# The last stage of a retrieval block: splits made in four column quarters, and another order of the sorted blocks

## The chip, the cores and the metric

The kernel runs on one core of one Trainium2 chip. Its time is the device time of one execution in microseconds (us), and the number that counts is the median over executions. The core has a matrix engine (PE, with PEld for the loads of its stationary operand), a vector engine (DVE), a scalar engine (ACT), GpSimd (POOL) and a queue engine (SP). SP and ACT start plain transfers between main memory and the on-chip memory SBUF; POOL starts the gathers whose row numbers are read from an on-chip table. Sixteen DMA engines move the bytes. Matrix products are summed in PSUM, in eight banks of 128 partitions by 512 fp32 numbers.

## The reference

The reference is one layer of an encoder on 256 tokens of width 2048: a mixer (short convolutions and latent attention) and then a retrieval FFN with 16384 single-neuron experts. Only the last part bears on this change. For each token eight heads choose 16 experts each, and

```python
u = u_tab[ids]
a = jnp.einsum('td,tnd->tn', hx, u)
act = jax.nn.gelu(a, approximate=False) * g
return jnp.einsum('tn,tnd->td', act, v_tab[ids])
```

The result is scaled by a gate, added to the residual `x`, and normalised: `y = RMSNorm(x + gate2 * PEER(h2))`.

## The kernel before

The table `u` is not gathered. All 128 blocks of 128 experts are multiplied with all tokens (main loop, `i1` from 0 to 127), the activations are weighed with the gates, and they are stored as rows of a table `actd`, one row of 256 tokens for each expert. Then comes the last stage, which this change touches.

For the product with `v` the kernel sorts the experts by which of eight groups of 32 tokens use them. The sorted list is cut into 109 blocks of 128 experts. For each block POOL issues one gather of 128 rows of `peer_v` (1 MB; tiles `rv`, `rvd`, `rvg`, `early`, `A`; line 1355) and one of the rows of `actd` that belong to them (128 KB, or 64 KB when only one half of the tokens needs the block; tiles `mc`, `mcs`; line 1366). These two alternate in POOL's queue, in the order of the table `ORDER`. Each gather waits for the eighth gather before it to have landed, and a gather into a reused tile waits for the last reader of that tile: a matrix product, or a split on DVE.

`plan()` turns `ORDER` into 89 turns of the matrix engine, numbered 0 to 88. A block is needed by groups of tokens; the tokens are in two halves (0 and 1). A turn is one of three kinds. A full turn multiplies all 128 tokens of one half with one block; it runs on reduced-precision operands, so the block and its activations are first split into a high and a low part, and the turn is three passes (high times high, low times high, high times low) of four products, one for each column quarter of 512. A pair turn takes two pieces of 64 tokens, a single turn four pieces of 32 tokens, in fp32 without a split. Half 0 is summed in the banks `po0` to `po3`, half 1 in `po4` to `po7`. Four blocks (`DEFER`) need only half 1, fully; they stand at the end of the turns as turns 85 to 88, and 86 to 88 are run column quarter by column quarter (`po4` first, all three turns, then `po5`, and so on).

The split is `split_to` (lines 245 to 247): ACT copies the source into the high part (line 246), then DVE subtracts the high part from the source (line 247). There are three pairs of split buffers (`hwhi0/hwlo0`, `hwhi1/hwlo1`, `hboth`), and two more (`hx`) near the end. `prepare` (line 1467) splits the block and then its activations (`mhl`); a fourth wait comes with that: a split waits until the full turns that used the pair are done.

After the turns, `finish` (line 1565) does for each half: product times gate into a temporary (1569), add to the residual (1570), square with a running sum on ACT (1571), the mean and the reciprocal root on 128 single numbers (1573 to 1579), multiplication with the weight `g_final` (1582), scaling by the root (1586 on ACT, 1588 on DVE), and two stores. The residual rows are loaded by SP (1544) into the tile `early` when its two halves are no longer needed for gathers, and `g_final` (1548) into the tile of an `rv` that was split.

The program's text is not the order on an engine: a scheduler places instructions of DVE and ACT by priority and by its own view of when operands are ready, so instructions of `finish` can stand ahead of a split. The products of the last stage and the gathers are kept in the order of the text. Each engine runs its own queue in order.

Of the kernel before, what the change touches and what calls it, by code (L numbers as in the profile page):

```python
# [44 lines left out]
NSORT = 109  # L45
PLACES = 256
SHIFT = 14
ORDER = (57, 86, 85, 47, 59, 106, 53, 58, 42, 98, 102, 1, 101, 34, 77, 8, 55, 16, 88, 10, 76, 5, 83, 107, 105,
# [4 lines left out]
DEFER = (78, 79, 80, 81)  # L53
SORT_FROM = 51
SORT_SIDE = 3.6
# [36 lines left out]
def plan():  # L92
# [3 lines left out]
    for m, n in rows + [(255, 128 * NSORT - BASE3)]:  # L96
        for b in range(at // 128, (at + n - 1) // 128 + 1):
            need[b] |= m
        at += n
    assert sorted(ORDER) == list(range(NSORT))  # L100
    assert all(need[b] == 240 for b in DEFER)
    turns, pairs, singles = [], [[], []], [[] for _ in range(4)]

    def emit(kind, lanes):
        turns.append([x.pop(0) + (kind,) for x in lanes if x])

    for n, b in enumerate(ORDER):
        for tt in range(2):
# [14 lines left out]
        for kind, lanes in (("pair", pairs), ("single", singles)):  # L123
            while all(lanes) or any(x and (last or x[0][0] <= n - HELD) for x in lanes):
                emit(kind, lanes)
    turns += [[(n, 1, "full")] for n, b in enumerate(ORDER) if b in DEFER]
    return turns, [need[b] for b in ORDER]

# [39 lines left out]
def hybrid_block_kernel(  # L168
# [53 lines left out]
    def keep(x):  # L222
        tc.keep_in_program_order(x)
        return x
# [20 lines left out]
    def split_to(src, hi, lo):  # L245
        S.activation(hi, src, AF.Copy)  # L246
        V.tensor_tensor(lo, src, hi.bitcast(F32), ALU.subtract)
# [1103 lines left out]
    def index(b):  # L1351
        return bass.IndirectOffsetOnAxis(ap=perm[:, b:b + 1], axis=0)

    def fetch_raw(kind, raw):
        keep(nc.gpsimd.indirect_dma_start(raw, None, v_rows, index(ORDER[len(raws)])))  # L1355
        raws.append(raw)
        kinds.append(kind)

    def fetch_m(m):
        n = len(ms)  # L1360
        to, at, rows = m, actd[:, :], index(ORDER[n])
        for h in range(2):
# [101 lines left out]
    def first(slots, ok=lambda x: True):  # L1464
        return slots.pop(min((x[0], k) for k, x in enumerate(slots) if ok(x))[1])

    def prepare(n, raw, m, gs):
        at, (hi, lo) = first(wide)
        also, k = first(narrow)
        mh, ml = mhl[:, 2 * k], mhl[:, 2 * k + 1]  # L1470
        ready[n] = max([at, also, taken.get(n, -1) + LANDS] + list(ready.values())) + 1.5
        split_to(raw, hi, lo)
        ts_ = slice(32 * gs[0], 32 * gs[-1] + 32)
        split_to(m[:, ts_], mh[:, ts_], ml[:, ts_])
        split[n] = (hi, mh), (lo, mh), (hi, ml)
        live.append((turn_of[1][n] if n >= 0 else -1, (hi, lo), k))

    for i in range(TAIL):
        m = ab[-1][:, ABLK - TAIL + i]
        if i:  # L1480
            prepare(-1, tails[i], m, range(8))
        for tt in range(2):
            for r, mm in split[-1] if i else [(tails[i], m)]:
                for d4 in range(4):
                    product(r, mm, tt, 128, d4, start=(i == 0))
# [14 lines left out]
    while i < len(turns):  # L1500
# [13 lines left out]
        while more:  # L1514
            more = False

            def usable(x):
                return not (x[1] == "T2" and len(raws) >= T2_STOP or x[1][0] == "W" and len(raws) >= W_STOP)

            if len(ms) < len(raws) and m_free:  # L1520
                fetch_m(first(m_free)[-1])
                more = True
            elif len(ms) == len(raws) < min(NSORT, now + AHEAD + 1) and any(map(usable, raw_free)):
                place = first(raw_free, usable)
                taken[len(raws)] = place[0]
                fetch_raw(*place[1:])
                more = True
            if seen < min(len(ms), now + SPLIT_AHEAD + 1) and (turn_of[1][seen] < 0 or wide and narrow):
                if turn_of[1][seen] >= 0:
                    prepare(seen, raws[seen], ms[seen], full_halves[seen])  # L1530
                held.append(seen)
                seen += 1
                more = True
            for n in [n for n in held if turn_of[0][n] < i]:
                held.remove(n)
                key = max(turn_of[0][n], ready.get(n, -1))
                raw_free.append((key, kinds[n], raws[n]))
                m_free.append((key, ms[n]))
                more = True
# [159 lines left out]
```

## Time and profile before

| | us |
|---|---|
| median of 3 executions | 1682.59 |
| lowest and highest | 1680.96, 1696.75 |
| the profiled execution | 1661.88 |
| its span | 1660.1 |
| matrix products of the last stage begin | 1314.9 |
| last gather issued by POOL | 1621.7 |
| split of the last gathered block begins on ACT | 1632.8 |
| last matrix product ends | 1646.3 |
| last arithmetic ends, last store is issued | 1654.5 |

The profile is of one execution, about 20 us shorter than the median of the others. In its rows L1444 is the line of all products of the last stage, whatever the kind of the turn, L246 and L247 are the two halves of a split, and a name such as `rv` stands for all tiles of that name. A row of the timeline gives the start, the duration and, in brackets, how long the engine had been idle and what ended that. A row with "x2" is two instructions merged into one row.

### The profile page before, as it was taken

To read this page: it belongs to the slowest core of one execution; us is meant where nothing else is said; L and a number is where in the kernel's file an instruction comes from. 1 tells how busy PE (TensorE), PEld (TensorE's weight loads), DVE (VectorE), ACT (ScalarE), POOL (GpSimd) and SP (SyncE) were. 2 spreads that over 40 slices of the span, in tenths; PEclk is the share of its full clock that TensorE was granted. 3 is DMA by queue.
4 is the path that set the end of the run, shared out by engine and by line. 5 is a ranking of instruction groups with operands and counts; after the bars stand their busy time and mean duration, and the time that the engine had idled before them with its cause. 6 is when DMAs were issued, how large, how long until landed. Compare 5 with 4: busy or idle time off the path is not lost.

```text
span 1660.1 us, 29785 instructions
## 1 busy us (share of the span) xinstructions
PE 1582.7 (95%) x12776; PEld 1384.5 (83%) x12780; DVE 1114.5 (67%) x1496; ACT 696.3 (42%) x787; POOL 471.4 (28%) x356
## 2 busy tenths in 40 slices
PE   3999999999999999999999999999999999898995
PEld 2779899999999999999999999999999866444432
DVE  5778778877777889998997866576675434123215
ACT  3225457534544446654664333434343333122113
POOL 0000000000000000000000006888885378777770
PEclk9999999999999999999999999999999999999997
DMA  9996988889665556655668779999999899999994
GB/s 394 426 418 234 348 330 328 302 307 339 233 244 178 185 203 204 232 201 205 253 225 286 237 270 268 288 358 359 341 354 397 297 344 363 388 400 381 374 417 198
DMA packets 115722, 502.52 MB, mean 303 GB/s; under 512 B 13392, under 2 KB 55888, under 8 KB 60288
## 3 DMA queue, kind: packets, MB, share of 16 engines
q1 hardware_dynamic: 44640, 319.79, 52.0%
q0 software_dynamic: 25184, 129.25, 20.2%
q10 hardware_dynamic: 45760, 51.51, 9.7%
q8 instruction: 102, 1.67, 0.4%
q14 instruction: 36, 0.29, 0.0%
HBM read 462.57 MB, written 37.94 MB: 301 GB/s over the span
## 4 chain that ended last, share of the span: by engine, by line
PE 79%; DVE 7%; DMA 6%; issue 3%; POOL 3%; ACT 2%; SPq 0%; DVEq 0%; ACTq 0%; POOLq 0%
PE pu L257 12%; PE pu L258 12%; PE pu L263 12%; PE po L1444 10%; PE pin L748 4%; PE pwin L257 2%; PE pwin L258 2%; PE pwin L263 2%; PE gps L1043 2%; PE pwout L257 2%; PE pwout L258 2%; PE pwout L263 2%; PE pq L258 2%; PE pq L257 2%; PE pq L263 2%
## 5 line engine op out<-in xcount | busy, mean ns | idle before, releaser
L257 PE MATMUL pu<-h2hi,hu 128*128 128x256 f32 x2048 | 479.7, 279 | 2.8 <-ACT hu L239 2.8
L239 ACT ACTIVATE hu<-ru 128x2048 fp32r<-128x2048 f32 x128 | 245.8, 1921 | 394.3 <-PE pu L258 291.2
L240 DVE TENSOR_TENSOR lu<-ru,hu 128x2048 fp32r<-128x2048 f32 x128 | 292.6, 2287 | 165.9 <-ACT hu L239 159.3
L257 PEld LDWEIGHTS pu<-h2hi,hu 128*128 128x128 f32 x2048 | 384.9, 188 | 3.5 <-ACT hu L239 3.2
L263 PE MATMUL pu<-h2hi,lu 128*128 128x256 f32 x2048 | 254.0, 277 | 0.9 <-DVE lu L240 0.9
L1320 POOL DMA_DIRECT2D gg<-gd x3 | 3.9, 1289 | 882.6 <-DMA permd<-pad 882.6
L1288 POOL DMA_INDIRECT permd<-work x126 | 207.0, 1643 | 148.7 <-DVE work L1284 110.6
L258 PE MATMUL pu<-h2loT3b,hu 128*128 128x256 f32 x1024 | 247.3, 278 | 0.0
L263 PEld LDWEIGHTS pu<-h2hi,lu 128*128 128x128 f32 x2048 | 242.1, 188 | 1.1 <-DVE lu L240 1.1
L258 PE MATMUL pu<-h2loT3a,hu 128*128 128x256 f32 x1024 | 240.4, 277 | 0.0
L258 PEld LDWEIGHTS pu<-h2loT3b,hu 128*128 128x128 f32 x1024 | 192.7, 188 | 0.2 <-issue 0.2
L258 PEld LDWEIGHTS pu<-h2loT3a,hu 128*128 128x128 f32 x1024 | 192.4, 188 | 0.0
L1444 PE MATMUL po<-rv,mc 128*32 128x512 f32 (+1 forms) x336 | 92.5, 604 | 0.0
L240 DVE TENSOR_TENSOR lwin<-rwin,hwin 128x2048 fp32r<-128x2048 f32 x33 | 75.5, 2288 | 22.2 <-ACT hwin L239 21.0
L1444 PE MATMUL po<-rv,mcs 128*32 128x512 f32 (+1 forms) x312 | 85.0, 600 | 5.7 <-DMA mcs<-actd,ident 4.3
L1355 POOL DMA_INDIRECT rv<-in_peer_v_dram,perm_idx x66 | 74.8, 1134 | 52.0 <-ACT hwhi L246 29.7
L239 ACT ACTIVATE hwin<-rwin 128x2048 fp32r<-128x2048 f32 x33 | 63.1, 1913 | 56.8 <-PE pin L748 26.6
L1444 PE MATMUL po<-hwhi,mhl 128*128 128x512 f32 x272 | 76.8, 410 | 6.0 <-ACT mhl L246 6.0
L257 PE MATMUL pwin<-hhi,hwin 128*128 128x256 f32 x336 | 81.0, 286 | 0.0
L258 PE MATMUL pwin<-hlo,hwin 128*128 128x256 f32 x336 | 78.7, 279 | 0.0
L1444 PEld LDWEIGHTS po<-hwhi,mhl 128*128 128x128 f32 x272 | 51.7, 194 | 29.0 <-ACT mhl L246 11.1
L284 DVE SCALAR_TENSOR_TENSOR acc<-ada,cact,acc 128x2048 f32<-128x2048 f32 x30 | 70.3, 2344 | 6.4 <-DMA ada<-in_w_ada_dram 6.4
(594 smaller groups left out, 3170.0 us busy)
## 6 DMA issues: line engine op xcount, KB each, us to landing
ru<-in_peer_u_dram SPq DMA_DIRECT2D x128, 1024.0 KB, 6.0
ada<-in_w_ada_dram SPq DMA_DIRECT2D x96, 1024.0 KB, 7.7
rwin<-in_w_in_dram SPq DMA_DIRECT2D x33, 1024.0 KB, 6.7
rwout<-in_w_out_dram SPq DMA_DIRECT2D x16, 1024.0 KB, 6.7
rwq<-in_w_q_dram SPq DMA_DIRECT2D x16, 1024.0 KB, 4.9
gd<-stage ACTq DMA_DIRECT2D x16, 1024.0 KB, 5.2
actd<-A ACTq DMA_DIRECT2D x14, 1024.0 KB, 8.8
gg<-gd ACTq DMA_DIRECT2D x13, 1024.0 KB, 8.0
```

The lines of the kernel that those rows point to most:

```text
L239: S.activation(hi, raw, AF.Copy)
L240: lo_op = V.tensor_tensor(lo, raw, hi.bitcast(F32), ALU.subtract)
L257: PE.matmul(dst, lhsT=whi[:, sl], rhs=rhi[:, c], start=(c == sets[0][0]), stop=False)
L258: PE.matmul(dst, lhsT=whi[:, sl], rhs=rlo[:, c], start=False, stop=False)
L263: PE.matmul(dst, lhsT=wlo[:, sl], rhs=rhi[:, c], start=False, stop=(c == cs[-1] and cs == last))
L284: op = V.scalar_tensor_tensor(acc, raw, cact[:, k:k + 1], acc, ALU.mult, ALU.add)
L748: PE.matmul(dst, lhsT=wt[:, (4 * n + j) * 128:(4 * n + j + 1) * 128], rhs=ht[:, 4 * q + j], start=start, stop=stop, skip_group_check=True)
L1043: keep(PE.matmul(p[:, j * 128:(j + 1) * 128], lhsT=ohs[0][:, t0 + j], rhs=ohs[1][:, t0 + j, c], start=(c == 0), stop=(c == 2)))
L1288: put_one = nc.gpsimd.indirect_dma_start(permd[:, :], bass.IndirectOffsetOnAxis(ap=place[:, i:i + 1], axis=0), ids[:, i:i + 1], None)
L1320: keep((S if 1 < k < NG - 1 else nc.gpsimd).dma_start(gg, gd[:, :, k * ABLK:(k + 1) * ABLK, :].rearrange("tb p i t -> p tb i t")))
L1355: keep(nc.gpsimd.indirect_dma_start(raw, None, v_rows, index(ORDER[len(raws)])))
L1444: keep(PE.matmul(po[tt * 4 + d4][row:row + size], lhsT=m[:, at * size:(at + 1) * size], rhs=raw[:, d4 * 512:(d4 + 1) * 512], start=start, ...
```

## The change

Two things. The split of a block is made in four pieces of 512 columns, each with its own ACT copy and its own DVE subtraction; the split of the activations stays one piece and still follows. And the table `ORDER` is another permutation of the same 109 blocks (same number of full, pair and single turns: 48, 21 and 20; the same bytes). In the new order the last turn that adds to half 0 is turn 82, before it was turn 84.

```diff
-ORDER = (57, 86, 85, 47, 59, 106, 53, 58, 42, 98, 102, 1, 101, 34, 77, 8, 55, 16, 88, 10, 76, 5, 83, 107, 105,
+ORDER = (82, 52, 45, 70, 84, 73, 85, 59, 86, 96, 2, 75, 6, 15, 50, 98, 38, 21, 61, 103, 19, 53, 5, 40, 34, 0,
 ...
         ready[n] = max([at, also, taken.get(n, -1) + LANDS] + list(ready.values())) + 1.5
-        split_to(raw, hi, lo)
+        for d4 in range(4):
+            ds_ = slice(d4 * 512, (d4 + 1) * 512)
+            split_to(raw[:, ds_], hi[:, ds_], lo[:, ds_])
         ts_ = slice(32 * gs[0], 32 * gs[-1] + 32)
         split_to(m[:, ts_], mh[:, ts_], ml[:, ts_])
```

Lines behind the insertion move down by two (1569 becomes 1571, 1582 becomes 1584). What the new order does on the engines shows at three places.

DVE at the end of the stage, before the change: the last two splits (`hwlo0`, `hx01`, with their `mhl`) and the start of `finish`.

```order
L247 TENSOR_TENSOR hwlo0_14790<-rvg_14832,hwhi0_14789 128x2048
L247 TENSOR_TENSOR mhl_14794<-mcs_14795,mhl_14794 128x128
L1569 TENSOR_TENSOR rvg_14832<-po0_14769,gtf_9852 128x512
L1569 TENSOR_TENSOR rvg_14832<-po1_14770,gtf_9852 128x512
L247 TENSOR_TENSOR hx01_16180<-rv4_14224,hx00_16179 128x2048
L247 TENSOR_TENSOR mhl_14794<-mcs_14795,mhl_14794 128x128
L1570 TENSOR_TENSOR early_13637<-early_13637,rvg_14832 128x512 x2
L1569 TENSOR_TENSOR rvg_14832<-po2_14771,gtf_9852 128x512
L1569 TENSOR_TENSOR rvg_14832<-po3_14772,gtf_9852 128x512
```

And after it, from the split of the block of turn 85 on.

```order
L247 TENSOR_TENSOR hwlo1_14792<-rvd1_14779,hwhi1_14791 128x512 x4
L247 TENSOR_TENSOR mhl_14794<-mcs_14795,mhl_14794 128x128
L1571 TENSOR_TENSOR A120_14294<-po0_14769,gtf_9852 128x512
L1571 TENSOR_TENSOR A120_14294<-po1_14770,gtf_9852 128x512
L1572 TENSOR_TENSOR early_13637<-early_13637,A120_14294 128x512 x2
L1571 TENSOR_TENSOR A120_14294<-po2_14771,gtf_9852 128x512
L1571 TENSOR_TENSOR A120_14294<-po3_14772,gtf_9852 128x512
L1572 TENSOR_TENSOR early_13637<-early_13637,A120_14294 128x512 x2
L1575 TENSOR_REDUCE fsum0_16481<-fs0_16479 128x1
L1576 TENSOR_SCALAR fv0_16483<-fsum0_16481 128x1
L1578 RECIPROCAL fr0_16485<-fr0_16485 128x1
```

Behind these stand three more small instructions of half 0, and only then the splits of the last three blocks (`hboth` from `rv6`, `hx01` from `rv7`, `hwlo0` from `rv5`), the four multiplications with `g_final` of half 0, and `finish` of half 1. So the sums and the root of half 0 moved ahead of three splits on DVE, and their squares and the root's ACT part moved ahead of the same splits on ACT.

PE around the last turns with half 0, after the change: `po0` to `po3` end with the third pass of turn 82 (its first and last products are shown), then the pair turn 83 and the single turn 84 add to half 1 alone.

```order
L1444 MATMUL po0_14769<-hwhi0_14789,mhl_14794 128x512
L1444 MATMUL po1_14770<-hwhi0_14789,mhl_14794 128x512
L1444 MATMUL po2_14771<-hwhi0_14789,mhl_14794 128x512
L1444 MATMUL po3_14772<-hwhi0_14789,mhl_14794 128x512
L1444 MATMUL po4_14773<-rv4_14224,mc0_14647 64x512
L1444 MATMUL po4_14773<-early_13637,mcs_14795 64x512
L1444 MATMUL po5_14774<-rv4_14224,mc0_14647 64x512
L1444 MATMUL po5_14774<-early_13637,mcs_14795 64x512
```

Before, the same kind of place was turn 84, a single turn whose pieces go to both halves.

```order
L1444 MATMUL po4_14773<-A120_14294,mc1_14648 32x512
L1444 MATMUL po0_14769<-rv3_14110,mc1_14648 32x512
L1444 MATMUL po4_14773<-rv3_14110,mc1_14648 32x512
L1444 MATMUL po0_14769<-rv7_14527,mcs_14795 32x512
L1444 MATMUL po5_14774<-A120_14294,mc1_14648 32x512
```

POOL in the middle of the stage, after the change: the gathers of the blocks 75 to 79 and of their activations, with the semaphores each waits for.

```order
L1355 DMA rvd1_14779<-in_peer_v_dram,perm_idx_5645 128x2048 [waits DMASW1_49,PE_49]
L1366 DMA mcs_14795<-actd_68,ident_70 128x128 [waits DMASW2_49,DVE_49]
L1355 DMA A120_14294<-in_peer_v_dram,perm_idx_5645 128x2048 [waits DMASW3_49,DVE_49,PE_49]
L1366 DMA mc3_14650<-actd_68,perm_idx_5645 128x256 [waits DMASW4_49]
L1355 DMA rv9_14781<-in_peer_v_dram,perm_idx_5645 128x2048 [waits DMASW5_49,PE_49]
L1366 DMA mcs_14795<-actd_68,perm_idx_5645 128x256 [waits DMASW6_49,DVE_49]
L1355 DMA early_13637<-in_peer_v_dram,perm_idx_5645 128x2048 [waits DMASW7_49,PE_49]
L1366 DMA mcs_14795<-actd_68,ones_71 128x128 [waits DMASW0_49]
L1355 DMA rvd1_14779<-in_peer_v_dram,perm_idx_5645 128x2048 [waits DMASW1_49,DVE_49]
```

The last row gathers block 79 into the tile `rvd1`, into which block 75 was gathered four blocks earlier; it waits on DVE for that block's split. Block 80 goes into the tile of block 76 in the same way. In the old order the shortest such distance was five blocks (42 into the tile of 37, 69 into that of 64).

8 rows, old and new, of the table ORDER are left out of this document.

## The prediction

> **What bounds the kernel now.** First the page's head and the stretches of the last stage (busy time of each engine with its number of instructions, granted clock, DMA share, GB/s).
>
> ```profile
> span 1660.1 us, 29785 instructions
> core 0: us, PE busy (x) PEld busy (x) DVE busy (x) ACT busy (x) POOL busy (x), PEclk, DMA share, GB/s
> 1310.00:1350.00 40.00, 40.00 (x221) 24.50 (x223) 16.15 (x15) 11.78 (x13) 30.63 (x26) 1.00 0.75 260
> 1350.00:1400.00 50.00, 50.00 (x265) 32.81 (x258) 20.29 (x15) 17.81 (x16) 40.25 (x33) 1.00 0.95 363
> 1400.00:1520.00 120.00, 112.24 (x597) 54.22 (x595) 25.34 (x20) 21.86 (x21) 92.65 (x85) 0.97 1.00 398
> 1520.00:1550.00 30.00, 29.10 (x132) 17.45 (x134) 12.60 (x10) 9.34 (x10) 24.82 (x18) 0.91 0.88 334
> 1550.00:1633.00 83.00, 73.36 (x396) 30.54 (x393) 18.75 (x15) 17.22 (x17) 56.20 (x52) 0.96 0.99 401
> 1633.00:1660.10 27.10, 10.63 (x36) 7.52 (x34) 20.72 (x42) 11.27 (x23) 0.00 (x0) 0.72 0.27 110
> ...
> 1309.60:1622.70 313.10, 297.07 (x1566) 156.11 (x1564) 89.74 (x72) 73.94 (x72) 244.85 (x210) 0.97 0.95 371
> ```
>
> Only the last 345 us change. To 1633 the DMA engines are nearly full, but not everywhere: 260, 363 and 334 GB/s stand beside 398 and 401. After 1633 DVE is the busy engine. What holds the DMA back is in POOL's rows (minimum, median and maximum in ns, then a stretch of its timeline) and DVE's for the same time.
>
> ```profile
> L1366 POOL DMA_INDIRECT mc<-actd,perm_idx x29: 942/946/2973, 1312.7 to 1608.7; - x29
> L1366 POOL DMA_INDIRECT mcs<-actd,perm_idx x24: 942/946/3035, 1327.6 to 1581.7; - x24
> POOL mcs L1366 <- issue: 14.9, 49, 0.3
> 1335.13 3.04 POOL L1366 DMA_INDIRECT mcs<-actd,perm_idx  x1 [0.30 <-issue]
> 1338.47 2.24 POOL L1355 DMA_INDIRECT A<-in_peer_v_dram,perm_idx  x1 [0.30 <-issue]
> 1341.01 1.89 POOL L1366 DMA_INDIRECT mcs<-actd,ones  x1 [0.31 <-issue]
> 1343.20 0.95 POOL L1355 DMA_INDIRECT rvg<-in_peer_v_dram,perm_idx  x1 [0.30 <-issue]
> 1351.97 0.94 POOL L1366 DMA_INDIRECT mc<-actd,ident  x1 [0.30 <-issue]
> 1335.06 2.29 DVE L247 TENSOR_TENSOR hwlo<-rv,hwhi 128x2048 fp32r<-128x2048 f32 x1 [1.37 <-ACT hwhi L246]
> 1337.27 0.42 DVE L247 TENSOR_TENSOR mhl<-mcs,mhl 128x256 fp32r<-128x256 f32 x1
> 1337.60 2.28 DVE L247 TENSOR_TENSOR hwlo<-rv,hwhi 128x2048 fp32r<-128x2048 f32 x1
> 1339.80 2.29 DVE L247 TENSOR_TENSOR hboth<-rv,hboth 128x2048 fp32r<-128x2048 f32 x1
> 1352.36 2.29 DVE L247 TENSOR_TENSOR hwlo<-rvd,hwhi 128x2048 fp32r<-128x2048 f32 x1 [1.51 <-ACT hwhi L246]
> ```
>
> Half of the gathers take 0.946 us, with 0.30 us between two. The long ones end 0.8 to 0.9 us behind the end of a wide subtraction: 1338.17 behind 1337.35, 1340.71 behind 1339.88, 1342.90 behind 1342.09. A gather that begins while a subtraction runs waits for its end, then takes its usual time, even though the next subtraction has begun: it slips in between two. The other way round there is no such wait: the subtraction of 1352.36 began inside the gather of 1351.97 and kept its 2.29 us.
>
> POOL's whole time is accounted for: 210 gathers of 0.946 us are 198.7 us, 209 gaps of 0.30 us are 62.7 us, and the busy time of 244.85 us is 46.2 us more than 198.7; sum 307.6 of 313.1 us. So it waits for tiles or landings for 5 us in all. The stage is paced by POOL's issue, of which 46 us is waiting for wide subtractions, and by the DMA engines where POOL runs ahead. Last, the end, from the last block's split on.
>
> ```profile
> 1632.77 1.92 ACT L246 ACTIVATE hx<-rv 128x2048 fp32r<-128x2048 f32 x1 [0.78 <-DMA rv<-in_peer_v_dram,perm_idx]
> 1635.44 2.28 DVE L247 TENSOR_TENSOR hx<-rv,hx 128x2048 fp32r<-128x2048 f32 x1
> 1637.78 1.02 PE L1444 MATMUL po<-hx,mhl 128*128 128x512 f32 x2 [2.34 <-DVE hx L247]
> 1639.05 1.28 DVE L1569 TENSOR_TENSOR rvg<-po,gtf 128x512 f32<-128x512 f32 x2
> 1642.31 1.28 ACT L1575 ACT_TABLE_LOAD   x1
> 1643.98 1.28 DVE L1569 TENSOR_TENSOR rvg<-po,gtf 128x512 f32<-128x512 f32 x2
> 1645.48 0.85 PE L1444 MATMUL po<-hx,mhl 128*128 128x512 f32 x3
> 1648.51 1.28 DVE L1570 TENSOR_TENSOR early<-early,rvg 128x512 f32<-128x512 f32 x2
> 1653.37 1.15 ACT L1586 ACTIVATE early<-early,fr 128x1024 f32<-128x1024 f32 x1 [0.81 <-DVE fr L1579]
> 1654.55 0.36 ACTq L1589 DMA_DIRECT2D out_dram<-early  x1
> ```
>
> Call L the landing of the last block, 1632.8. PE's last product ends at 1646.3, L+13.6; the last arithmetic at 1654.5, L+21.7; the span at L+27.3. DVE begins half 1 only at 1643.98, because the sums of half 0 and a split stood in its queue before that.
>
> **The change part by part.** The first and the last wide subtraction of POOL's time, and the durations of a split's pieces:
>
> ```profile
> 1309.73 2.29 DVE L247 TENSOR_TENSOR hwlo<-rvd,hwhi 128x2048 fp32r<-128x2048 f32 x1 [1.52 <-ACT hwhi L246]
> ...
> 1615.83 2.29 DVE L247 TENSOR_TENSOR hwlo<-rvd,hwhi 128x2048 fp32r<-128x2048 f32 x1 [5.42 <-ACT hwhi L246]
> ...
> L246 ACT ACTIVATE mhl<-mcs x19: 289/294/420, 1332.8 to 1634.6; 128x128 fp32r<-128x128 f32 x12, 128x256 fp32r<-128x256 f32 x7
> L246 ACT ACTIVATE hwhi<-rv x9: 1894/1911/1915, 1333.1 to 1534.3; 128x2048 fp32r<-128x2048 f32 x9
> L247 DVE TENSOR_TENSOR hwlo<-rvd,hwhi x7: 2291/2291/2294, 1309.7 to 1615.8; 128x2048 fp32r<-128x2048 f32 x7
> ```
>
> *One split.* ACT's copy grows by (1.911-0.294)/1920 us a column, so 512 columns take 0.62 us, and four some 2.3 us instead of 1.9. Two 512-wide DVE operations last 1.28 us and the next row shows the same shape 1.2 us on, so 0.60 us each: four are 2.4 instead of 2.29 us. But a quarter's subtraction follows its own copy: the low part is ready about 3.0 us after the landing instead of 4.3. The high part of the activations, which ACT makes after the copies, comes 0.4 us later. PE meets both; off the end this moves nothing, as POOL's queue sets the pace. [...]
>
> *POOL's waits.* 35 wide subtractions lie between 1309.7 and 1622.7 (the first and the last are quoted above), so each costs POOL 1.3 us. Four quarters keep DVE busy for 2.4 us, in which POOL, at 1.25 us plus a wait, begins about 1.5 gathers; each waits for the rest of one quarter, 0.30 us on average. That is 0.46 us a split, 16 us in all: 30 us saved in POOL's queue. Bounds: 46 us if no gather meets a quarter badly; 4 us if two gathers wait a whole quarter each time (2x0.60x35 = 42).
>
> *What of it reaches the end.* With POOL ahead, the DMA engines are next. From 1350 to 1633 the rows give 363x50+398x120+334x30+401x83 = 109.2 MB; at 400 GB/s (the two full stretches) that takes 273 us instead of 283: 10 us. From 1310 to 1350 small gathers come first and POOL's rate counts; of the three waits shown (2.1, 1.3 and 0.9 us), a third would stay: some 2 us of the 40. So L comes 12 us earlier. Bounds: nothing (400 GB/s is only reached where it was), and 20 us, if the faster POOL fills the DMA as in its best stretches.
>
> *The order.* Same blocks, same bytes, same kinds of turns. It could make PE late or starve it; the trace of before cannot show it, so I bound it by the stage's PE slack: PE was busy 73.36 of the last 83 us and 112.24 of 120, some 17 us idle. I take 0, with 5 us either way. The gather that waits for a split only four blocks back (block 79) has three blocks in flight before it, 1.1 MB each at 400 GB/s, 8 us; its split needs 3. Nothing is lost there.
>
> *The end.* Half 0 is complete at turn 82; eight 512-wide DVE operations (4.8 us), a square on ACT, the 1.28 us table load and a few small ones, 8 us in all, now run before the last three blocks land. Before, blocks came 2.8 us apart at the end (1.1 MB at 400 GB/s), so block 101, which turn 82 needs, lands near L-20 and turn 82 ends near L-15: room for 8 us before the split at L-5.6. In queue behind this on DVE and ACT are the last three splits, and PE behind those; if the cover were gone, each us late costs one at the end. Then: last split ready at L+3.3 (was 1637.7, L+5.0); PE needs the 8.5 us it took from 1637.78 to 1646.3, so L+11.8; meanwhile DVE does `g_final` for half 0 and half 1's first columns. After the last product: product, one `g_final` piece and sum, 1.8 us; from the last sum to the end of arithmetic 4.0 us (4.7 before, from 1649.8 to 1654.5, with more `g_final` pieces in it); the store 5.5 us as before. L+23, not L+27.3: 4.5 us, between 2 and 6.
>
> Sum: 12+4.5 = 16.5 us: 1661.9 becomes 1645.4 for a profiled execution, and carried over as the same number of us, the median 1682.6 becomes 1666. Why the median lies 20 us above the profiled execution the trace doesn't show.
>
> **The rivals.**
>
> 1. *Only the end is gained.* The DMA share of 0.95 from 1309.6 to 1622.7 can be read as full already: POOL then merely waits for landings instead of subtractions. For it: 0.99 to 1.00 at 398 and 401. Against it: 260, 363 and 334 GB/s where the long gathers crowd. L gains 0 to 4, the end 4.5: 1676. [...]
>
> 2. *More is gained.* POOL's 30 us reach L nearly whole, the DMA running above 401 GB/s: L-20, end -6: 1657.
>
> 3. *Slower: gathers and quarters take turns.* If whichever begins first holds off the other, each quarter can wait for a gather, three more waits a split of about half of 0.94 us: 1.4 us a split. POOL gains nothing, since it waits for each quarter. Splits on the path pay: those that PE waited for
>
> ```profile
> PE po L1444 <- ACT mhl L246: 8.1, 3, 4.4
> PE po L1444 <- DVE hwlo L247: 2.9, 4, 0.9
> ```
>
> seven times 1.4, and three at the end, 14 us, less 4.5: 1692. It decides if a quarter's duration grows beyond 0.7 us. Against it stands the subtraction of 1352.36.
>
> **How the numbers follow.** Forecast 0.60, rival 1 0.22, rival 2 0.10, rival 3 0.08. The forecast's own range is 1659 to 1675 (L by 5 to 18, the end by 2 to 6). For 8 in 10 I take 1651 to 1681: it holds the first three, with a few us for the spread of the medians (1680.96 to 1696.75). A measurement tells about 1% from no change, 1665.8 to 1699.4 here; the forecast lies on that line. Over 1% faster: 0.10 from rival 2, half of the forecast, 0.04 from rival 1 by spread: 0.45. Slower by over 1% needs rival 3 and more: 0.06. The rest, 0.49, is within.
>
> **What would show it.** POOL's gathers longer than 1.6 us are gone and its busy time over them falls from 245 to about 215 us; 260, 363 and 334 GB/s rise towards 400; the last gather is issued 12 us sooner. Squares of half 0 stand before the splits of the last three blocks, the table load off the path, the end at L+23. Wrong: POOL's mean gather unchanged; quarters of 0.7 us or more; new POOL waits on PE; the half-0 sums running after L.

## The result, and the profile after

The changed kernel's median is 1686.94 us (1678.27 to 1842.26, 21 executions), that of the kernel before 1680.96 us in the same comparison (1666.70 to 1698.75, 21 executions). The ratio is 1.0063 with a 95% interval of 1.0040 to 1.0086: slower, by about 11 us by the ratio and 6 us by the medians. Slow executions, such as the one of 1842.26 us, are left out of the ratios here and below. The forecast was 1666, with a range of 1651 to 1681. The profiled execution of the changed kernel took 1684.45 us, close to its median.

First the head of its page, and then the stretches, with the columns of the prediction: busy time of PE, PEld, DVE, ACT and POOL with their instructions, granted clock, DMA share, GB/s. The last row covers POOL's 210 gathers.

```profile
span 1682.6 us, 30095 instructions
```

```profile
1310.00:1350.00 40.00, 35.11 (x150) 18.41 (x149) 13.70 (x26) 12.14 (x28) 26.29 (x28) 0.91 0.76 273
1350.00:1400.00 50.00, 49.47 (x273) 25.45 (x273) 16.33 (x29) 13.56 (x28) 31.74 (x32) 1.00 0.93 358
1400.00:1520.00 120.00, 111.13 (x537) 53.22 (x535) 33.50 (x60) 29.35 (x60) 73.07 (x77) 0.97 0.92 364
1520.00:1550.00 30.00, 27.02 (x144) 9.92 (x140) 5.79 (x11) 5.77 (x12) 17.42 (x19) 0.97 0.89 341
1550.00:1633.00 83.00, 76.37 (x350) 42.31 (x351) 28.15 (x50) 24.23 (x49) 50.98 (x54) 0.91 0.96 373
1633.00:1660.00 27.00, 25.62 (x158) 11.92 (x156) 11.70 (x26) 10.69 (x24) 4.08 (x5) 1.00 0.63 233
...
1308.88:1638.56 329.68, 305.79 (x1486) 153.66 (x1488) 98.59 (x177) 86.17 (x176) 204.66 (x210) 0.95 0.91 352
```

POOL's gathers are no longer stretched: 204.66 us instead of 244.85, 6.0 us above 210 times 0.946. Yet they are spread over 329.68 us instead of 313.10, and the DMA moves less, not more (364 GB/s where it was 398). POOL now waits, and PE has a wait that it did not have (us in total, times, longest).

```profile
POOL rv L1355 <- PE po L1444: 27.6, 11, 7.2
POOL early L1355 <- DVE hwlo L247: 9.2, 2, 5.0
POOL early L1355 <- PE po L1444: 6.3, 3, 4.6
PE po L1444 <- issue: 23.0, 26, 2.2
```

POOL waits for tiles that PE has not finished with. PE itself is idle for 23.0 us, in 26 pieces, with no releaser that the profile shows ("issue"). The first pieces stand in PE's timeline of turn 1, a single turn, on tiles that earlier products of the same turn had read already. The row below is POOL's, for the gather into a tile that this turn holds:

```profile
1331.29 0.60 PE L1444 MATMUL po<-early,mc 128*32 128x512 f32 x2
1333.30 0.59 PE L1444 MATMUL po<-rv,mc 128*32 128x512 f32 x1 [1.41 <-issue]
1336.10 0.79 PE L1444 MATMUL po<-rv,mc 128*32 128x512 f32 x1 [2.21 <-issue]
1337.53 1.01 PE L1444 MATMUL po<-rv,mc 128*32 128x512 f32 x1 [0.64 <-issue]
1338.92 1.86 PE L1444 MATMUL po<-early,mc 128*32 128x512 f32 x2 [0.38 <-issue]
1341.03 1.01 PE L1444 MATMUL po<-early,mc 128*32 128x512 f32 x1 [0.24 <-issue]
...
1343.16 1.35 POOL L1355 DMA_INDIRECT early<-in_peer_v_dram,perm_idx  x1 [4.58 <-PE po L1444]
```

PE's starts lie 2.8, 1.4, 1.4 and 2.1 us apart: multiples of 0.7. Product by product PE is held for a multiple of that; then the granted clock falls (0.56 from 1337 to 1344, 0.91 in the stretch's row) and a product takes 1.01 instead of 0.59 us. The idle time without a releaser is not in the profile of before, which was the ground of the prediction.

### The profile page after: what moved, and what is told of

Its sections match the earlier page's. It is cut to its first block, busy times and chain, and to the rows that moved or that the text cites. A ratio compares the mean times of both kernels' runs of the same rounds, so it can differ in the third digit from the quotient of the medians.

```text
span 1682.6 us, 30095 instructions
## 1 busy us (share of the span) xinstructions
PE 1601.0 (95%) x12776; PEld 1386.6 (82%) x12780; DVE 1125.6 (67%) x1610; ACT 708.1 (42%) x901; POOL 427.7 (25%) x356
## 4 chain that ended last, share of the span: by engine, by line
PE 83%; DVE 6%; issue 4%; DMA 3%; ACT 2%; SPq 0%; DVEq 0%; ACTq 0%
PE po L1444 19%; PE pu L257 11%; PE pu L258 11%; PE pu L263 11%; PE pin L748 4%; DMA ru<-in_peer_u_dram 3%; PE pwin L257 2%; PE pwin L258 2%; PE pwin L263 2%; PE gps L1043 2%; PE pwout L257 2%; PE pwout L258 2%; PE pq L258 2%; PE pwout L263 2%; PE pq L257 2%
## 5 line engine op out<-in xcount | busy, mean ns | idle before, releaser
L1444 PE MATMUL po<-rv,mc 128*32 128x512 f32 (+1 forms) x392 | 118.8, 618 | 10.7 <-issue 10.2
L1355 POOL DMA_INDIRECT rv<-in_peer_v_dram,perm_idx x65 | 64.2, 988 | 86.4 <-DMA actd<-A 28.4
L1444 PEld LDWEIGHTS po<-rv,mc 128*32 128x32 f32 (+1 forms) x392 | 29.3, 121 | 62.6 <-issue 62.6
L247 DVE TENSOR_TENSOR hwlo<-rv,hwhi 128x512 fp32r<-128x512 f32 x48 | 30.5, 693 | 69.5 <-ACT hwhi L246 44.6
```

The lines of the kernel that those rows point to most:

```text
L1444: keep(PE.matmul(po[tt * 4 + d4][row:row + size], lhsT=m[:, at * size:(at + 1) * size], rhs=raw[:, d4 * 512:(d4 + 1) * 512], start=start, ...
```

## The experiments

The runs fell on three chips, which I call A (e1 to e4), B (e5 to e15) and C (e16 to e18). The chips of the first timing and of the first profile of before are not recorded. Ratios are to the kernel before, run beside the others on the same chip, with 95% intervals.

**The parts apart, on chip A.** e1 takes the new split and the old table, e2 the new table and the old split:

```diff
 # e1: ORDER as before
-        split_to(raw, hi, lo)
+        for d4 in range(4):
+            ds_ = slice(d4 * 512, (d4 + 1) * 512)
+            split_to(raw[:, ds_], hi[:, ds_], lo[:, ds_])
 # e2: split_to(raw, hi, lo) as before, and
-ORDER = (57, 86, 85, ...
+ORDER = (82, 52, 45, ...
```

> The old order with the quarter splits. Theory Q (the quarters gain what POOL's rows promised, the new order costs more than that): 6 to 14 us faster than before (ratio 0.992 to 0.996), long gathers gone, no wait of POOL for a product above 5 us in all, last gather issued 8 to 14 us sooner than 1621.7. Theory O (the order is harmless, the quarters themselves cost, as more and smaller instructions): 4 to 10 us slower (ratio 1.002 to 1.006), and the new idle time of PE without a releaser (23 us in the profile of the changed kernel) is here too. Theory N (POOL's saving is hidden by the full DMA engines, and the idle time of PE is chance): ratio 0.998 to 1.002.

> The new order with whole splits. Theory Q: 12 to 20 us slower than before (ratio 1.007 to 1.012), with POOL waiting over 20 us for products and landings at places where a tile of a block four turns back is needed again, and its gathers long beside the wide subtractions as before. Theory O: within 4 us of before, since the bytes and the turns are the same. Theory N: 4 to 8 us slower, about what the whole change costs.

e3 is e1 with `range(2)` and 1024 columns a piece.

> The old order with splits in two halves of 1024 columns. By my reading of POOL's waits a gather that meets a half waits 0.6 us on average, and about 1.5 gathers start in a split: some 30 us of waits in all instead of 46, 15 us saved where the quarters save 30. Theory Q: about half of the gain of the quarters, 3 to 7 us faster than before. Theory O: about half of the quarters' loss, 1 to 4 us slower. Theory N: no change, within 3 us.

e4 is the changed kernel, unaltered.

> The changed kernel once more, unaltered, for a second profile. If the idle time of PE without a releaser (26 times, 23 us, on a grid of 0.7 us, at 1331 to 1343 and at 1432 to 1466 and 1546 to 1571) belongs to the kernel, it is here at the same places with 15 to 30 us. If it is chance of the one execution, it is below 8 us or at other places, and the span is some 10 to 20 us shorter than 1682.6.

Measured, with 1667.41 us for the kernel before: e1 1636.99, ratio 0.9806 (0.9769 to 0.9843); e2 1667.53, ratio 0.9984 (0.9954 to 1.0014); e3 1645.15, ratio 0.986 (0.9819 to 0.990); e4, one execution, 1637.07. So on chip A the quarters gained 32 us by the ratio (30 by the medians) and the halves about seven tenths of it, the order nothing that can be measured, and the one execution of the changed kernel was 30 us faster than before's median. None of the three theories had this: the gain of the quarters is more than twice the most that theory Q gave them, theory O had them slower, and the order costs nothing, as theory O alone had it. No profile of this chip has PE idle without a releaser, so the idle time does not belong to the kernel by itself. The rows over the 210 gathers and some stretches of e4:

```profile
1350.00:1400.00 50.00, 50.00 (x298) 26.77 (x300) 16.42 (x29) 14.38 (x29) 36.69 (x39) 1.00 1.01 411
1400.00:1520.00 120.00, 120.00 (x680) 58.34 (x672) 34.10 (x61) 30.13 (x62) 82.44 (x86) 1.00 1.01 415
1520.00:1550.00 30.00, 30.00 (x134) 18.88 (x132) 13.08 (x24) 11.28 (x24) 23.16 (x23) 1.00 1.01 409
...
1310.85:1603.45 292.60, 287.98 (x1581) 153.21 (x1580) 104.37 (x189) 89.91 (x187) 204.50 (x210) 1.00 0.99 398
```

The same row of e3, the halves:

```profile
1312.00:1606.49 294.49, 287.98 (x1558) 152.66 (x1556) 91.43 (x107) 77.44 (x105) 218.29 (x210) 0.99 0.98 393
```

POOL's waiting for subtractions is 46.2 us with whole splits, 19.6 with halves, 5.8 with quarters. In the stretches shown of e4 (1350 to 1550) the DMA engines run at 409 to 415 GB/s and PE is busy without a break.

**Chance or chip?** e5 is the changed kernel, e8 the kernel before, both unaltered; e6 and e7 cut one half of the split each, with the old order:

```diff
 # e6
+        S.activation(hi, raw, AF.Copy)
         for d4 in range(4):
             ds_ = slice(d4 * 512, (d4 + 1) * 512)
-            split_to(raw[:, ds_], hi[:, ds_], lo[:, ds_])
+            V.tensor_tensor(lo[:, ds_], raw[:, ds_], hi[:, ds_].bitcast(F32), ALU.subtract)
 # e7: the four copies S.activation(hi[:, ds_], raw[:, ds_], AF.Copy), then one subtraction of 2048 columns
```

> The changed kernel, unaltered, timed beside the kernel before on one chip. Two results stand against each other: the first timing (6 us slower than before, ratio 1.006) and the single execution of 1637.1 us beside a median of 1667.4 of before (30 us faster). Theory K (the difference hangs on the chip or its condition, through idle time of PE that no semaphore explains: 23 us of it in the first profile, none in the second): either some 30 us faster (ratio 0.981 to 0.985) with a profile in which that idle time is below 3 us, or within 10 us of before with over 10 us of it; nothing between. Theory L (the single execution was luck): ratio 0.995 to 1.008 and no such idle time.

> The old order; ACT copies the whole block in one instruction as before, and only DVE's subtraction is cut into four. Theory W (POOL's gathers wait for wide subtractions, and that is the whole gain): like the quarter splits alone, 24 to 32 us faster than before (ratio 0.981 to 0.986). Theory S (the gain is that the low part of a split is ready 1.3 us sooner, so that PE and the tiles come free sooner): less than 5 us faster, since the subtraction cannot start before the whole copy is there.

> The old order; ACT copies the block in four quarters, and DVE subtracts it in one instruction of 2048 columns as before. Theory W: no gain, 0 to 4 us slower than before (the copies take 0.3 to 0.4 us more a split), gathers stretched to 2 to 3 us as before and POOL's gather time at about 245 us. Theory S: nothing gained either, since the subtraction waits for the last copy; so W and S are told apart by the run with cut subtractions, and this one says whether ACT's pieces matter at all.

> The kernel before, unaltered, for a second profile on this chip. Theory W: POOL busy 240 to 250 us over the 210 gathers, some 35 of them above 1.6 us, DMA 330 to 400 GB/s with stretches below 350, and PE throttled to half its clock behind each wait of over 2 us, as in the first profile.

Measured on chip B: e5 1685.6 against 1674.89, ratio 1.0085 (1.0044 to 1.0127), the first result once more; e6 1.0021 (0.9989 to 1.0054), where theory W had 24 to 32 us of gain, e7 1.0023 (0.9987 to 1.0060). All have PE's idle time (e6 27.8 us, e7 21.9), the kernel before too. PE's wait in e5:

```profile
PE po L1444 <- issue: 23.8, 24, 1.7
```

And in e8:

```profile
PE po L1444 <- issue: 14.2, 21, 1.5
```

Theory K held in its mechanism, that the difference hangs on the chip or its condition, though the loss is 14 us by the ratio (11 by the medians) where it had at most 10. On e8 I was wrong: I expected a profile like the first one, with PE waiting for named work; it has 1.0 us of named waits and 14.2 us of the others. The half clock that I expected there stood in the last stage of the first profile of before behind its four waits of over 2 us (4.41, 2.17 with 0.91 soon after it, 4.26 and 2.34 us; granted clock 0.50 to 0.56 over the 3.0 to 3.6 us from 1520.85, 1593.86, 1624.97 and 1637.78). In e8 PE has no wait in that stage of over 1.5 us.

**The parts apart, on a chip with the idle time; and half of the bytes.** e9 and e10 are e1 and e2 again. e11 is the changed kernel with

```diff
-        keep(nc.gpsimd.indirect_dma_start(raw, None, v_rows, index(ORDER[len(raws)])))
+        keep(nc.gpsimd.indirect_dma_start(raw[:, :1024], None, v_halves, <twice the row number>))
```

from the tenth block on, where `v_halves` is the table seen as rows of 1024.

> The quarter splits with the old order a second time. Its profile says on which kind of chip these runs are: with PE's unexplained idle time (20 us or more in 20 to 30 pieces on a grid of 0.7 us) or without. Without: 26 to 32 us faster than before again. With it, theory P (PE, with its stalls, is the bound there, so what POOL saves changes nothing): 0 to 6 us slower than before, from a few more pieces of idle time; theory O2 (the new order is what costs 10 to 14 us on such a chip, the quarters still gain): 3 to 10 us faster than before.

> The new order with whole splits a second time. On a chip without PE's idle time: within 5 us of before again. On a chip with it: theory O2 expects 6 to 14 us slower than before; theory P expects within 5 us.

> The changed kernel, but from the tenth block on a gather brings only the first 1024 columns of each row; products and splits of the right half read the left half instead, so PE, ACT, DVE and POOL have as many instructions of the same sizes as before, and the DMA engines about half of the bytes (some 230 GB/s). The right half of the result is wrong by that. Theory D (on a chip with PE's idle time, it comes while the DMA engines are full): that idle time falls below 5 us, PE's products from the first to the last take 300 to 310 us, and POOL is the pace. Theory C (the idle time is PE's own on such a chip, whatever the DMA does): 15 us or more of it stay, 24 pieces or so. On a chip without the idle time this run says nothing on either.

They fell on chip B: e9 0.9964 (0.9908 to 1.0020), e10 1.0020 (0.9977 to 1.0063). Both have PE's idle time (24.2 and 16.7 us). Quarters alone are not slower there, the order alone is not measurably slower, and neither theory is clearly told from the other: e9 is what O2 expected, e10 what P expected. PE's wait in e11, and its long stretch:

```profile
PE po L1450 <- issue: 23.3, 28, 2.3
```

```profile
1400.00:1520.00 120.00, 113.00 (x554) 54.92 (x548) 33.76 (x60) 29.00 (x60) 73.95 (x77) 1.00 0.66 200
```

At 200 GB/s PE is held as long as at 364. Theory D, full DMA engines, fell.

**Without gathers.** e12 is the changed kernel, e13 and e14 are e6 and e7 again. e15 is the changed kernel with all gathers of the last stage replaced by loads of contiguous rows from SP:

```diff
-        keep(nc.gpsimd.indirect_dma_start(raw, None, v_rows, index(ORDER[len(raws)])))
+        keep(nc.sync.dma_start(raw, v_rows[ORDER[len(raws)] * 128:(ORDER[len(raws)] + 1) * 128]))
 # and the same for the rows of actd
```

> The changed kernel once more, to tell on which kind of chip this call runs. Without PE's unexplained idle time: 26 to 34 us faster than before, from PE's first product of the stage to the landing of the last block some 295 us, tail 22 us. With it: 5 to 15 us slower, 325 to 332 us, tail above 35 us.

> One ACT copy, four DVE subtractions, old order, a second time. Without PE's idle time, theory W (POOL waits for wide subtractions): 22 to 30 us faster than before, POOL's gather time below 215 us. Theory S (sooner readiness of the low part): under 5 us. With the idle time: within 6 us of before, as the first time, which decides nothing.

> Four ACT copies, one DVE subtraction, old order, a second time. Without PE's idle time both theories: 0 to 4 us slower than before, gathers stretched as before. A gain of over 5 us here would say that ACT's pieces have a part in it that I do not see. With the idle time: within 6 us of before.

> The changed kernel with plain loads of contiguous rows by SP in place of all gathers of the last stage (same bytes and tiles; the rows are not the sorted ones, so the result is another), and no work for POOL there. On a chip with PE's idle time: theory G (it comes from the gathers' descriptors or from POOL's own instructions) expects it below 5 us; theory C (it is PE's own on such a chip) 15 us or more. On either chip the stage shows what is left when POOL is not the pace: with the DMA engines as the limit, 115 MB at 415 GB/s, 275 to 285 us to the landing of the last block; with PE as the limit 300 to 310 us.

Chip B again: e12 1.0060 (1.0015 to 1.0106), e13 1.0023 (0.9973 to 1.0074), e14 0.9979 (0.9937 to 1.0022), with 22.8, 27.5 and 21.7 us of PE's idle time. e15, one execution, has none in the last stage; its stage began 45 us later than e4's (PE waited 35.0 us at one place of the main loop, probably because the early loads stood ahead of the main loop's on SP), so its total is not to be compared. All of PE's waits in the stage, and the rows of the stage:

```profile
PE po L1443 <- ACT mhl L246: 0.5, 1, 0.5
PE po L1443 <- DVE mhl L247: 0.2, 1, 0.2
```

```profile
1400.00:1520.00 120.00, 120.00 (x677) 63.86 (x679) 42.14 (x77) 36.24 (x74) 0.00 (x0) 1.00 1.02 415
1362.90:1658.90 296.00, 295.22 (x1594) 155.70 (x1593) 108.99 (x199) 92.32 (x192) 0.00 (x0) 1.00 0.98 392
```

With the same tiles, products and splits, at 415 GB/s, PE does its stage on chip B in 296 us (300 to 310 expected). So on that chip the idle time goes with POOL's gathers: theory G, not C.

The same execution has some of it earlier, in the main loop, 4.1 us in seven places. POOL's row there is that of the sort, which writes 128 row numbers at a time to main memory by an indirect transfer:

```profile
PE pu L258 <- issue: 2.3, 3, 0.8
PE pu L263 <- issue: 1.4, 3, 0.8
PE pu L257 <- issue: 0.4, 1, 0.4
1021.53 0.52 PE L263 MATMUL pu<-h2hi,lu 128*128 128x256 f32 x3 [0.81 <-issue]
...
1177.43 0.39 PE L257 MATMUL pu<-h2hi,hu 128*128 128x256 f32 x1 [0.42 <-issue]
L1288 POOL DMA_INDIRECT permd<-work x126 | 190.9, 1515 | 148.6 <-DVE work L1284 110.5 <-issue 37.8 <-DMA permd<-work 0.3
```

All seven places lie between 1021.5 and 1177.4, and POOL issues the 126 transfers from 1005.6 to 1233.7. e12 has 6.4 us in its main loop, the first profile of the changed kernel, e6, e8 and e14 less than 1 us each, all of it inside the same stretch of POOL; the other runs on B have none there, and the runs on A and C none either. So the idle time comes with POOL's indirect transfers, small ones too, and needs neither rows of 8 KB nor the last stage. What it is in them that holds PE is not shown.

**Which half of the split, on chip C.** e16 and e17 are e6 and e7 a third time. e18 replaces the large gathers alone by plain loads (as in e15, from the tenth block on) and leaves the small ones on POOL.

> One ACT copy, four DVE subtractions, old order. On a chip without PE's idle time: theory W 22 to 30 us faster than before (ratio 0.982 to 0.987), theory S under 5 us. On a chip with it: within 6 us of before for the third time.

> Four ACT copies, one DVE subtraction, old order. On a chip without PE's idle time: both theories within 4 us of before. On a chip with it: within 6 us of before.

> The changed kernel, in which from the tenth block on the 1 MB of a block comes by a plain load of contiguous rows from SP (not the sorted rows, so the result is another), and only the 109 small gathers of the activations stay on POOL. On a chip with PE's idle time, theory G1 (it goes with the number of gathers that POOL issues): 8 to 14 us of it stay. Theory G2 (it needs the gathers of 8 KB rows): below 3 us. Theory G3 (any gather in flight will do): 20 us or more. On a chip without it, none, and the run says only what the stage takes when POOL issues half as much: 285 to 296 us from PE's first product to the last landing.

Chip C is without the idle time. e16: 0.9833 (0.9765 to 0.9902), 1638.12 against 1668.38 us. e17: 0.9971 (0.9934 to 1.0009), an interval that holds 1. The rows over the 210 gathers, e16 and then e17:

```profile
1306.10:1599.30 293.20, 289.30 (x1581) 154.03 (x1579) 98.60 (x178) 76.03 (x72) 206.30 (x210) 0.99 0.98 398
```

```profile
1312.25:1625.32 313.07, 295.91 (x1557) 155.36 (x1555) 89.52 (x71) 83.84 (x174) 245.94 (x210) 0.98 0.95 370
```

Cut subtractions alone free POOL and give the gain; cut copies alone do neither. Theory W is shown where PE has no such idle time, and theory S is out. e18 (1632.38 us, one execution) says nothing on the idle time here; with half of POOL's gathers gone PE's products take 298.8 us from first to last, of which it is busy 296.3. So with quarters the stage is near PE's own limit: in e4 they take 305.8.

## Why the prediction was wrong

**What the forecast rested on.** "PE was busy 73.36 of the last 83 us and 112.24 of 120, some 17 us idle": the slack that was to take up any lateness of PE. It was read in a profile without the held products. On a chip with them, PE has no slack: between its first and last product of the stage the changed kernel takes 357.4 us in its first profile (1313.9 to 1671.3) and 305.8 in e4. PE is the bound, POOL waits for PE's tiles (the 27.6 us above), and what POOL saves cannot reach the end. This is the failed step: that POOL's queue sets the pace, so that 12 us of its saving reach L, and that PE's slack makes everything else 0. Of the 22.5 us between the spans of the two profiles, 15.9 had come by the end of POOL's last gather (1638.56 against 1622.70) and 6.6 came behind it, where 12 and 4.5 were to be gained. On chip B the cut subtractions free POOL as well (210 gathers in 207.4 us in e6 and 209.6 in e13, 245.7 in e8) and nothing is gained (1.0021, 1.0023).

The idle time that the profile shows is the smaller part of PE's loss. The two stages differ by 51.6 us; PE's idle time in them, named waits included, differs by 20 us (26.4 against 6.5), and PE's busy time makes up the rest (331.0 against 299.3). While products are held, pieces that otherwise run side by side (four start between 1329.11 and 1329.13 in the first profile) run one by one (1333.30, 1336.10 and 1337.53), some of them at the lower clock (1.01 instead of 0.59 us). The 32 products of turn 1 take 14.3 us in the first profile, 4.9 of them shown as idle, and 3.6 in e4. The first product of turn 1 and of the turn behind it, in the first profile and then in e4:

```profile
1329.11 0.62 PE L1444 MATMUL po<-rv,mc 128*32 128x512 f32 x1
1343.42 0.64 PE L1444 MATMUL po<-early,mc 128*64 128x512 f32 x1
...
1333.05 0.62 PE L1444 MATMUL po<-rv,mc 128*32 128x512 f32 x1
1336.62 0.64 PE L1444 MATMUL po<-early,mc 128*64 128x512 f32 x1
```

No rival held this: I listed "new POOL waits on PE" as a sign of error without pricing it. Rival 3's 1692 lies nearest to what was measured, but by chance: it had POOL gain nothing and the splits pay 1.4 us each, while POOL's gathers fell from 244.85 to 204.66 us and a split of four quarters still takes 2.50 us. The hint stood in my own text: the median lay 20 us above the profiled execution, and I said the trace doesn't show why. On chip B the kernel before had medians of 1674.9 to 1680.5 us and 14.2 us of PE's idle time in its profile, on A and C 1667.4 and 1668.4. The three times given ahead are the first three of the 21 of the comparison, and the profile of the changed kernel is the first of its 21, with the idle time. So the times and the profile of before that I was given probably come from different conditions; for that profile this is inferred, not shown.

**The mechanism on POOL was right.** Subtractions of 2048 columns hold up gathers, quarters hardly do: with copies in four pieces and whole subtractions (e17) the 210 gathers take 245.94 us, with whole copies and cut subtractions (e16) 206.30.

**Its size was off.** "each waits for the rest of one quarter, 0.30 us on average", 16 us in all: measured 5.8. And the DMA engines, which I capped at 400 GB/s, ran at 409 to 415 in e4 (1350 to 1550), where POOL kept ahead. For L, 12 us were predicted; in e4 the gathers take 20.5 us less (292.60 instead of 313.10). On A it went as rival 2 had it (1657, 25 us below the median): 30 to 32 us. The price of a quarter was right: a median of 0.69 us, four in 2.50 (2.4 predicted), four copies 2.19 (2.3). Rival 3 had 0.7 us as its point of decision. 39 of the 156 quarters of e4 are above that, but none above 0.75, where 1.4 us a split would be 0.35 for each; so its mechanism is out. Rival 1 is out on A: L, where the last split begins, is 1613.4 in e4 and was 1632.8.

**The order.** "I take 0, with 5 us either way": 0.9984 on A holds it. The two timings of the changed kernel on B (1.0085 and 1.0060) agree with the first one (1.0063, on an unknown chip), while quarters alone gave 0.9964. So beside the quarters the order costs some 16 to 20 us there by the middle values (the interval of e9 alone is 9 us to either side), though by itself (e10) the ratio is 1.0020. The tail of the first profile shows one part. Start, duration, and idle time before, if any:

```profile
1645.80 1.29 DVE L1571 TENSOR_TENSOR A<-po,gtf 128x512 f32<-128x512 f32 x2 [15.88 <-PE po L1444]
1648.21 0.63 ACT L1573 ACTIVATE A<-early 128x512 f32<-128x512 f32 x1 [19.27 <-DMA rv<-in_peer_v_dram,perm_idx]
...
1653.26 0.20 ACT L1577 ACTIVATE fr<-fv 128x1 f32<-128x1 f32 x1
1653.37 2.18 ACT L246 ACTIVATE hboth<-rv 128x512 fp32r<-128x512 f32 x4
...
1658.08 0.74 PE L1444 MATMUL po<-hx,mhl 128*128 128x512 f32 x2 [0.66 <-ACT mhl L246]
1659.53 0.51 PE L1444 MATMUL po<-hx,mhl 128*128 128x512 f32 x1 [0.71 <-DVE mhl L247]
...
1664.01 1.48 PE L1444 MATMUL po<-hx,mhl 128*128 128x512 f32 x3
...
1669.75 0.87 PE L1444 MATMUL po<-hx,mhl 128*128 128x512 f32 x3
```

PE finishes half 0 so late that `finish` starts at 1645.80; the squares stand in ACT's queue ahead of the last three splits, and `hboth` starts at 1653.37 with no idle time before it, though the gathers' bytes had come by about 1646 (29 GB/s from 1646 to 1648). PE then waits for the splits, and its products fall to half of the clock: 1.48 us for three, later 0.87 (granted clock 0.52 from 1660.3 to 1667.2). That is the case I named, "if the cover were gone, each us late costs one at the end", without a chance for it. No wait there was longer than 0.76 us; PE was busy for 1.66 of the 3.30 us before 1660.3, so here the lower clock came behind a stretch that was half idle. How the rest of the order's cost comes about is open.

**The end** was right where PE is not late. In e4 the squares and the table load are done by 1603.4, and the last split starts at L:

```profile
1601.87 1.28 ACT L1577 ACT_TABLE_LOAD   x1
1603.16 0.20 ACT L1577 ACTIVATE fr<-fv 128x1 f32<-128x1 f32 x1
...
1613.42 2.19 ACT L246 ACTIVATE hwhi<-rv 128x512 fp32r<-128x512 f32 x4 [0.28 <-DMA rv<-in_peer_v_dram,perm_idx]
```

The span is 1635.3, L+21.9 (L+23 predicted). In e1, with the old order, it is L+26.9 (1611.80 to 1638.7). The end is so 5.0 us shorter, but e4's stage began 1.9 us later, and the two spans differ by 3.4 us. Beside the median of e1, 1636.99 us, e4 with its 1637.07 gains nothing: that the end is worth something in the time is not shown on A either.

## What to carry to other kernels

Cut wide two-input DVE instructions where GpSimd issues gathers beside them: four of 512 columns instead of one of 2048 gave 30 us of 1667 on the two chips where PE had room for it, and nothing on the third. Before an engine's idle time is counted as slack, see that the profile and the times come from the same conditions; a gap between the profiled execution and the median is a term of the sum, not a footnote. Work moved ahead of a split in an in-order queue is free only as long as the engine that releases it is not late: in the first profile of the changed kernel the split of `hboth` began at 1653.37, with its bytes there by about 1646.

## What the hardware showed that I had not expected

On one of three chips PE is held between products, with no releaser in the profile (starts 2.1 and 1.4 us apart in e11, multiples of 0.7 as in the first profile of the changed kernel): 14 to 28 us of shown idle time in each of the ten runs with gathers there (e5 to e14), none in the seven runs on the two other chips, and none in the last stage of e15, which has no gathers there. Half of the bytes did not change it (23.3 us). Small indirect transfers in the main loop are enough to bring some of it (4.1 us in e15). Whether it is the chip or what went on beside the kernel, and how it grows with the number or the size of the transfers, was not settled; the run that was to tell the latter (e18) fell on a chip without it. By this the quarters gain 1.9% on A, the cut subtractions 1.7% on C, and the whole change loses 0.6 to 0.9% on B. The scatter differs as well: on A the kernel before lay between 1662.18 and 1686.83 us, that with quarters between 1635.86 and 1640.60.
